# A decoder block with Strassen steps: a longer warm-up, two host units and the last branch unit with other step kinds, and operand fills spread over more ticks

## The chip, the core and the metric

The kernel runs on one core of one Trainium2 chip, as a single program. The metric is the device time of that program in microseconds (us). Three runs of the kernel before took 2395.96, 2396.16 and 2397.62 us; their median is 2396.16 us.

The engines go by their names in the profile: PE is TensorE (matmul; PEld is its weight load), DVE is VectorE, ACT is ScalarE, POOL is GpSimd and SP is SyncE. [...] A q behind a name (SPq, ACTq) marks what the engine's sequencer issues, DMAs above all.

## What is computed

One layer over 256 tokens of 4096 channels, float32:

```
h = rmsnorm(x, norm_w)
u_p, z_p, u_c, b_c, c_c, z_c, g = split(h @ w_in)     # 6 x 2048 and 8192 columns
pooled = trailing_mean(u_p, windows 2, 4, 8, 16) - u_p # by group of 512 channels
y_pool = (pooled @ pool_w) * pool_scale * silu(z_p)
v      = c_c * u_c
y_conv = b_c * (conv_b + sum_k conv_w[k] * shift(v, 2 - k)) * silu(z_c)
br     = y_pool @ w_branch[0], y_conv @ w_branch[1]
merged = sum over n of sigmoid(g_n + gate_b[n]) * br_n
out    = rmsnorm(x + merged @ w_out, final_norm_w)
```

Almost all of the work is in three matrix products with 256 rows: 4096 x 20480 (w_in), twice 2048 x 4096 (w_branch) and 4096 x 4096 (w_out).

## The kernel before

**Units and steps.** The columns of every weight matrix are cut into units of 1024 columns (class Unit, L332). The units run in this order: conv units cz0, cb0, cu0, cc0, cz1, cb1, cu1, cc1; pool units pz0, pu0, pz1, pu1; gate units g0_0, g1_0 to g0_3, g1_3; branch units b0_0, b1_0 to b0_3, b1_3; output units o0 to o3. A unit goes over its contraction dimension in steps of 256 rows (16 steps for w_in and w_out, 8 for a branch). One step multiplies a 256 x 256 block of the activations by a 256 x 1024 block of weights, 1 MB, which SP loads into one of three slots of `raw`.

Each float32 number is split into a rounded high part and a low part, and a product is done as high x high + high x low + low x high. A step has one of two kinds, given by a letter in the unit's text (L34 to L43):

- P, plain: eight products of 128 x 128 by 128 x 512, three matmuls each, 24 in all. ACT writes the weights' high parts into cells of `ring` (`highs`), DVE the low parts (`lows`).
- S, a Strassen step: seven products, 21 matmuls. DVE first makes four sums of the weights in `parts` (one addition of 128x1024, two of 128x512), ACT rounds the three used quarters of `raw` and the four sums, DVE subtracts for both.

Two more letters stand in the text of a host unit (HOST, L40): B is a step of banded matmuls for the trailing means, and M a step that multiplies them by pool_w. pz1 and g0_0 are the host units.

**The order of the work.** All of it is written out by hand: every engine call goes through `pin`, which keeps the program order of each engine. While PE's matmuls are issued, `pump` (L901 on) adds the preparation of the next steps to the other engines, up to four steps ahead (AHEAD), as far as ring cells and raw slots are free. After every six matmuls a `tick` (L927 on) takes one item from `queue`, which holds the epilogue of the unit before (activations, transposes, stores, with None as a pause), and calls `pop_fill` (L726).

**Activation operands.** The stationary side lies in `arena` (and `last_pair`), high and low part, for P operands the four blocks, for S operands also the sums that Strassen's method needs. For w_in it is made from x in the opening. Later ones, of y (branch) and of the merged result (output), are fills: class Fill, L695 on. A fill loads one block from DRAM by POOL's queue into one of two stage buffers, sa or sb; LANDING ticks later, when its place in the arena is free, `advance` does one phase in each tick: for an S operand the four subtractions of `sums_s` on DVE, then a copy on DVE (L687) and a subtraction on DVE; for a P operand a copy on ACT and a subtraction on DVE. If a step begins whose operand isn't ready, `run_step` forces the fill in front of it.

**End of a unit.** ACT evacuates the four banks of `sums` as they close (`evacuate`, L368), DVE combines the Strassen corners into them (`combine`, L389), and the next unit may write a bank only when it is evacuated.

**The convolution's taps** (`c_epi`, L490 on) run in the epilogue of cc0 and cc1, so beside the steps of cz1 and pz0: four lots of four instructions on DVE (128x255 and 128x254) with two on ACT, then a load of b's factor to E (`g_d`), six ticks later the product into Y, and two stores of Y to `y_d`.

**The opening** (L777 on). DVE clears `warm`, ACT starts the load of the parameters `par` and runs a small activation on `warm`, and PE multiplies `warm` ten times (WARM). SP loads the first weights in four parts of 256 KB, with the first block of x (256 KB, `fetch_x(0)`) issued after the first part. `x_direct` scales x on ACT (two instructions) and subtracts on DVE (two); for the first two steps ACT's `highs` and DVE's `lows` are done part by part.

Of the kernel before, what the change touches and what calls it, by code (L numbers as in the profile page):

```python
# [27 lines left out]
NRAW = 3  # L28
AHEAD = 4
TICK = 6  # L30
WARM = 10
TAIL = 3

SIX5 = "PPPPPSPSPSPSPSPS"  # L34
# [2 lines left out]
SIX4 = "PPPPSPSPSPSPSPSP"  # L37
SEVEN3 = "PPPSPSPSPSPSPSPS"
EIGHT = "PSPSPSPSPSPSPSPS"
HOST = "PPPBPPMMPPSPSSPSSPS"  # L40
OUT3 = "PSPSPSPSPSPSSPPP"
B0 = "PPPPSPSP"
B1 = "PSPSPSPP"  # L43


@with_exitstack
def hybrid_block(ctx: ExitStack, tc: tile.TileContext, x, xc, prm, rows_in, w_in, pool_w, w_branch, w_out, out):
    nc = tc.nc
# [4 lines left out]
    def act(dst, src, func=AF.Copy, **kw):  # L53
        return pin(nc.scalar.activation(dst, src, func, **kw))  # L54
# [4 lines left out]
    def mul(dst, a, b):  # L59
        return tt(dst, a, b, ALU.mult)  # L60
# [9 lines left out]

    def load(dst, src):
        return pin(nc.sync.dma_start(dst, src))

    def move(dst, src):
        return pin(nc.gpsimd.dma_start(dst, src))
# [129 lines left out]
    def highs(cells, src):  # L205
        for i, c in runs(cells):
            act(ring[:, c, 0], src[:, i])
# [14 lines left out]
    class Step:  # L222
# [7 lines left out]
        def first(self):  # L230
            if self.kind == "B":
                return []

            def rounded(cells):
                self.q = self.raw.rearrange("p (i c) -> p i c", i=4)
                self.cells = cells
                if self in steps[:2]:
                    for i in range(4):
                        highs(cells[i:i + 1], self.q[:, i:i + 1])
                else:  # L240
                    highs(cells, self.q[:, 0:len(cells)])

            return [(3 if self.kind == "S" else 4, None, rounded)]
# [145 lines left out]
    def combine(u):  # L389
        d = u.dst  # L390
        if u.s:
            corner_sums(u)
            assert u.cornered
            q = u.join.slot.rearrange("p (n t) c -> p t n c", n=2)
            d4 = d.rearrange("p t (n c) -> p t n c", n=2)
            if u.scaled:
                for t in range(2):
                    stt(d4[:, t], q[:, t], rin[:, t:t + 1], d4[:, t], ALU.mult, ALU.add)
            else:
                add(d4, d4, q)  # L400
            u.join.prepared = True
        u.flags["base"] = True
        if u.urgent:
            u.urgent()

# [25 lines left out]
    def put(dst, src):  # L431
        for k in range(2):
            move(dst[:, :, 1 - k], src.rearrange("p (q k) t -> p q k t", k=2)[:, :, k])

    def chan(tile_):
        return tile_.rearrange("p a n -> p (a n)").rearrange("p (b t) -> p b t", t=T)
# [4 lines left out]
    def gap(n):  # L441
        return [None] * n
# [5 lines left out]
    def make_ops(kinds):  # L448
# [2 lines left out]
    x_ops = make_ops([("P" if r[0] == "p" else "S", r) for r in x_regions])  # L451
    y_ops = [make_ops([("P", ("p", i)) for i in range(6)] + [("S", ("s", i)) for i in (0, 1)]),
             make_ops([("P", r) for r in (("p", 6), ("p", 7), ("q", 0), ("q", 1), ("q", 2))] +
                      [("S", ("s", i)) for i in (4, 5, 6)])]
    m_ops = make_ops([("P" if r[0] == "p" else "S", r) for r in x_regions])

    def sequence(text, np_, total, both):
# [24 lines left out]
    def conv_units(c, first):  # L482
        base = 2 * HALF + c * NU

        def b_epi(u):
            def copy(j):
                act(chan(Y)[:, 2 * j:2 * j + 2], bankview(j))
            return gap(6) + transposes(E, copy) + [lambda: move(g_d[c], Y)]

        def c_epi(u):  # L490
            def copy(j):
                if j == 3:
                    for i in range(4):
                        act(chan(E)[:, 2 * i:2 * i + 2], bankview(i))

            def taps(j):
                v, y = chan(E)[:, 2 * j:2 * j + 2], chan(Y)
                for i in range(2):
                    b = 2 * j + i
                    kb = 8 * c + b  # L500
                    act(y[:, b], v[:, i], AF.Identity, scale=tap_col(2, kb), bias=bias_col(kb))
                for i in range(2):
                    b = 2 * j + i
                    kb = 8 * c + b
                    for s in (1, 2):
                        stt(y[:, b, s:], v[:, i, 0:T - s], tap_col(2 - s, kb), y[:, b, s:], ALU.mult, ALU.add)

            items = gap(6) + pairs(transposes(E, copy)) + gap(1)
            for j, n in enumerate((1, 5, 7, 7)):
                items += gap(n) + [lambda j=j: taps(j)]  # L510
            return items + [lambda: move(E, g_d[c])] + gap(6) + [lambda: mul(Y, Y, E), lambda: put(y_d[1, c], chan(Y))]

        in_unit(f"cz{c}", base + 3 * HALF, lambda u: silu_y(), FIRST if first else SIX4, dst=Y)
        in_unit(f"cb{c}", base + HALF, b_epi, EIGHT).urgent = lambda: mul(E, E, Y)
        in_unit(f"cu{c}", base, lambda u: gap(2) + band_items(0) if c == 0 else [], SEVEN3, dst=Y)
        in_unit(f"cc{c}", base + 2 * HALF, c_epi, EIGHT).urgent = lambda: mul(E, E, Y)
# [115 lines left out]
    def branch_unit(n, c):  # L632
        def epi(u):
            if n == 0:
                return gap(8) + [lambda: mul(Y, E, Y)]
            turned = spare() if c < 3 else Y

            def gated():
                mul(E, E, spare())
                if c == 3:  # L640
                    last_pair["stack"].close()
                    open_last(F32R)
                    last_pair["again"] = True

            def copy(j):
                act(chan(turned)[:, 2 * j:2 * j + 2], bankview(j))

            def stored():
                put(m_d[c], chan(turned))
                merged[c] = now[0] + STORED  # L650
            return [lambda: move(spare(), gates_d[1, c])] + gap(6) + [gated, lambda: add(E, E, Y), None,
                lambda: c < 3 and move(Y, gates_d[0, c + 1])] + gap(3) + pairs(transposes(E, copy)) + [stored]

        text = B1 if n else B0
        u = Unit(f"b{n}_{c}", lambda i: w_branch[n, c, i], seq_y(text), y_ops[n], epi)
        u.urgent, u.lead, u.rotates = (lambda: None), 3, False
        units.append(u)
# [28 lines left out]
    def copy(dst, src):  # L686
        return pin(nc.vector.tensor_copy(dst, src))  # L687
# [7 lines left out]
    class Fill:  # L695
        def __init__(self, o, src, free, ready):
            self.o, self.free, self.ready, self.src = o, free, ready, src
            self.at = self.st = None
            self.phase = 0

        def fetch(self, st):
            self.at, self.st = now[0], st
            move(st[:, 4:8].rearrange("p o c -> p (o c)"), self.src)

        def advance(self):
            o, q = self.o, self.st[:, 0:self.o.n] if self.o.kind == "S" else self.st[:, 4:8]
            if self.phase == 0 and o.kind == "S":
                sums_s(self.st)
                self.phase = 1
            elif self.phase == 0:  # L710
                act(o.view[:, 0], q)
                self.phase = 2
            else:
                if self.phase == 1:
                    copy(o.view[:, 0], q)
                sub(o.view[:, 1], q, o.view[:, 0].bitcast(F32))
                self.phase = 3
                o.ready = True
                fills.remove(self)

    stages = [sa]
    fills = deque()
    now = [0]
    LANDING, STORED = 8, 7

    def pop_fill(force=None):  # L726
        now[0] += 1
        for f in list(fills):
            if f.at is not None and f.free() and (now[0] >= f.at + LANDING or f.o is force):
                f.advance()  # L730
                break
        used = [f.st for f in fills if f.at is not None]
        nxt = next((f for f in fills if f.at is None), None)
        if nxt is None or not nxt.ready():
            return
        st = next((q for q in stages if not any(q is u for u in used)), None)
        if st is not None:
            nxt.fetch(st)
# [38 lines left out]
    warm = op.tile([P, 2 * P], BF16, name="warm")  # L777
    pin(nc.vector.memset(warm, 0.0))
    pin(nc.scalar.dma_start(par, prm))
    act(warm[:, 0:2], warm[:, 2:4])  # L780
    make_identity(nc, ident)
    for _ in range(WARM):
        pin(nc.tensor.matmul(shared(3)[:, 0:2 * P], warm[:, 0:P], warm, start=True, stop=True))
# [22 lines left out]
    xt = Y.rearrange("p a n -> p (a n)").rearrange("p (s o c) -> p s o c", s=4, c=P)  # L806

    def fetch_x(j):
        load(xt[:, j % 4].rearrange("p o c -> p (o c)"), xc[first_order[j]])

    staged = [j for j in range(16) if x_ops[first_order[j]].kind == "S"]

# [71 lines left out]
    def issue_load(s):  # L884
        i = s.load_index
        r = raw[:, i % NRAW]
        if isinstance(s, Join):
            s.slot = r.rearrange("p (i c) -> p i c", i=4)
            return
        if i < 2:  # L890
            for k in range(4):
                load(r[:, k * NH:(k + 1) * NH], s.src[:, k * NH:(k + 1) * NH])
                if i == k == 0:
                    fetch_x(0)
        else:
            load(r, s.src)
        if i + 1 < 16:
            fetch_x(i + 1)
        s.raw = r
# [45 lines left out]
    def after_group(u, b, st):  # L945
# [14 lines left out]
            state["limit"] = state["now"] + u.lead  # L960
        pump()

    pump()

    def room(o):
# [166 lines left out]
```

## Time and profile before

| | us |
|---|---|
| median of three runs | 2396.16 |
| the profiled execution, its own time | 2395.7 |
| its span, first to last instruction | 2394.0 |
| matmuls in it | 10,515 |
| mean granted TensorE clock | 0.997 |
| DMA | 547 MB, 229 GB/s in the mean |

The rows that follow come from four views. The list of waits gives, for one engine, who released it, the total, the number and the longest. The timeline gives start, duration, engine, source line, operation, output <- input, shape, how many instructions are merged in the row, and in square brackets the engine's idle time before it with the releaser. The table of stretches gives for each stretch its length, then busy time and number of instructions of PE, PEld, DVE, ACT and POOL, then the granted clock, the DMA engines' share and GB/s. The chain of waits follows the end back from releaser to releaser. Durations overlap a little: a row of 33 matmuls lasts to the end of the last, while the next row starts when PE issues again.

### The profile page before, as it was taken

The numbers are of one execution on the slowest core, as the hardware profiler recorded it, in microseconds if no ns is written. First come the engines' busy times: TensorE is split into PE (matmuls) and PEld (weight loads), VectorE is DVE, ScalarE is ACT, GpSimd is POOL, SyncE is SP. The second block draws the span as 40 slices with busy tenths as digits, with TensorE's granted clock in tenths as the row PEclk, the third lists the DMA queues.
The fourth block names the chain that finished last, engine by engine and source line by source line (L and its number), as shares of the span: only waits on it lengthen the run. The fifth ranks groups of instructions, "written<-read, shape, count | busy, mean of one in ns | idle before, by whom it ended". The sixth has DMA issues, their size and how long they took to land. (4 is left out here: it accounts for less than half of the span.)

```text
span 2394.0 us, 26867 instructions
## 1 busy us (share of the span) xinstructions
PE 2372.0 (99%) x10515; PEld 1956.6 (82%) x10515; DVE 2136.9 (89%) x1770; ACT 1421.8 (59%) x1368; POOL 85.7 (4%) x147
## 2 busy tenths in 40 slices
PE   9999999999999999999999999999999999999998
PEld 7888888888888888888888888888888887888886
DVE  8779989988989969969998899889998798899998
ACT  6655556655556556556666656556665555556664
POOL 0000000000000000000000000001100001000000
PEclk9999999999999999999999999999999999999999
DMA  9656546655646645645766676677776766757767
GB/s 346 234 179 238 190 182 243 230 195 201 223 176 227 233 182 196 234 177 210 260 233 210 245 242 233 198 251 263 238 283 219 261 233 220 254 194 268 254 216 268
DMA packets 83391, 547.07 MB, mean 229 GB/s; under 512 B 9536, under 2 KB 9536, under 8 KB 22336
## 3 DMA queue, kind: packets, MB, share of 16 engines
q1 hardware_dynamic: 69824, 485.52, 56.0%
q0 software_dynamic: 13008, 58.73, 8.4%
q8 instruction: 82, 1.34, 0.2%
q10 hardware_dynamic: 432, 1.11, 0.1%
q14 instruction: 45, 0.37, 0.1%
HBM read 519.10 MB, written 26.21 MB: 228 GB/s over the span
## 5 line engine op out<-in xcount | busy, mean ns | idle before, releaser
L939 PE MATMUL sums<-ring,arena 128*128 128x512 f32 x7515 | 1751.5, 390 | 6.3 <-DVE ring L57 2.9
L939 PEld LDWEIGHTS sums<-ring,arena 128*128 128x128 f32 x7515 | 1409.2, 188 | 302.9 <-DVE ring L57 4.6
L57 DVE TENSOR_TENSOR ring<-raw,ring 128x1536 fp32r<-128x1536 f32 (+3 forms) x528 | 938.6, 1789 | 142.8 <-ACT ring L54 139.0
L54 ACT ACTIVATE ring<-raw 128x1536 fp32r<-128x1536 f32 (+3 forms) x528 | 790.7, 1515 | 460.3 <-PE sums L939 286.5
L54 ACT ACTIVATE ring<-parts 128x1024 fp32r<-128x1024 f32 (+1 forms) x402 | 400.6, 1010 | 391.4 <-DVE parts L57 331.6
L939 PE MATMUL shared<-ring,arena 128*128 128x512 f32 x2100 | 507.1, 390 | 1.2 <-DVE ring L57 1.2
L57 DVE TENSOR_TENSOR ring<-parts,ring 128x2048 fp32r<-128x2048 f32 (+3 forms) x224 | 434.8, 1953 | 42.6 <-ACT ring L54 41.8
L939 PEld LDWEIGHTS shared<-ring,arena 128*128 128x128 f32 x2100 | 395.2, 188 | 85.0 <-DVE ring L57 2.6
L57 DVE TENSOR_TENSOR parts<-parts,raw 128x512 f32<-128x512 f32 x378 | 261.9, 693 | 12.9
L57 DVE TENSOR_TENSOR parts<-raw 128x1024 f32<-128x1024 f32 x189 | 230.6, 1220 | 7.1 <-DMA raw<-in_w_in_dram 7.0
L939 PE MATMUL sums<-ring,last_pair 128*128 128x512 f32 x366 | 89.8, 396 | 0.0
L939 PEld LDWEIGHTS sums<-ring,last_pair 128*128 128x128 f32 x366 | 68.9, 188 | 16.5
L54 ACT ACTIVATE E<-sums,rin 128x512 f32<-128x512 f32 x56 | 36.3, 688 | 25.5 <-PE sums L939 25.4
L57 DVE TENSOR_TENSOR raw<-raw 128x512 f32<-128x512 f32 (+1 forms) x42 | 36.5, 869 | 10.3 <-ACT raw L54 9.3
L939 PE MATMUL shared<-ring,last_pair 128*128 128x512 f32 x168 | 41.6, 396 | 0.0
L939 PEld LDWEIGHTS shared<-ring,last_pair 128*128 128x128 f32 x168 | 31.6, 188 | 7.7
L54 ACT ACTIVATE raw<-shared 128x512 f32<-128x512 f32 x56 | 29.7, 610 | 0.4 <-DVE ring L57 0.2
L57 DVE TENSOR_TENSOR E<-E,last_pair 128x2048 f32<-128x2048 f32 x12 | 27.4, 2285 | 2.7 <-ACT E L54 2.7
L78 POOL DMA_DIRECT2D E<-in_rows_dram x16 | 13.9, 867 | 444.3 <-DVE E L69 442.2
L54 ACT ACTIVATE last_pair<-shared 128x512 f32<-128x512 f32 x44 | 24.1, 596 | 7.7 <-PE shared L422 7.0
L54 ACT ACTIVATE E<-sums 128x512 f32<-128x512 f32 x44 | 25.6, 599 | 4.0 <-PE sums L939 1.4
L54 ACT ACTIVATE Y<-shared 128x512 f32<-128x512 f32 x44 | 23.8, 598 | 4.8 <-PE shared L422 4.7
(120 smaller groups left out, 602.9 us busy)
## 6 DMA issues: line engine op xcount, KB each, us to landing
raw<-in_w_in_dram SPq DMA_DIRECT2D x318, 1024.0 KB, 4.8
raw<-in_w_branch_dram SPq DMA_DIRECT2D x64, 1024.0 KB, 4.9
raw<-in_w_out_dram SPq DMA_DIRECT2D x64, 1024.0 KB, 4.9
E<-in_rows_dram POOLq DMA_DIRECT2D x16, 512.0 KB, 8.1
gates_d<-E POOLq DMA_DIRECT2D x8, 1024.0 KB, 8.0
Y<-in_xc_dram SPq DMA_DIRECT2D x16, 256.0 KB, 6.6
raw<-in_pool_w_dram SPq DMA_DIRECT2D x4, 1024.0 KB, 6.8
Y<-gates_d POOLq DMA_DIRECT2D x4, 1024.0 KB, 5.8
```

What stands on the lines that cost most here:

```text
L54: return pin(nc.scalar.activation(dst, src, func, **kw))
L57: return pin(nc.vector.tensor_tensor(out=dst, in0=a, in1=b, op=op))
L78: return pin(nc.gpsimd.dma_start(dst, src, accum_op=ALU.add))
L939: pin(nc.tensor.matmul(ps, lhs, rhs, start=n == 0, stop=n == u.total[b] - 1))
```

## The change

- WARM is 18 instead of 10. The small activation on `warm` is gone.
- The first block of x is loaded by ACT's DMA queue (`feed`), ahead of the first `pump`; SP issues the four parts of the first weights one behind the other.
- In the first step, the high part of the first quarter of the weights is a copy on DVE instead of an activation.
- HOST has nine P and seven S instead of ten and six; its S steps begin one place sooner.
- The last branch unit, b1_3, has the text B1_LAST: S at places 2 and 5 instead of 2, 4 and 6. Operand 5 of that branch is used by a P step there, and is laid in the region s6, which has room for all eight blocks.
- The pauses ahead of the four lots of taps are 1, 7, 9, 9 ticks instead of 1, 5, 7, 7. The product goes into E instead of Y and is stored from E.
- Fills: an S operand's copy is on ACT; at least four ticks lie between its sums and the copy, and one between copy and subtraction; for five ticks after a unit's `combine` (QUIET), `advance` starts no phase but the copy of an S operand.

```diff
-WARM = 10
+WARM = 18
...
-HOST = "PPPBPPMMPPSPSSPSSPS"
+HOST = "PPPBPPMMPSPSSPSSPSS"
...
+B1_LAST = "PSPPSPPP"
...
+    def feed(dst, src):
+        return pin(nc.scalar.dma_start(dst, src))
...
                     for i in range(4):
-                        highs(cells[i:i + 1], self.q[:, i:i + 1])
+                        if self is steps[0] and i == 0:
+                            copy(ring[:, cells[0], 0], self.q[:, 0])
+                        else:
+                            highs(cells[i:i + 1], self.q[:, i:i + 1])
...
         u.flags["base"] = True
+        quiet[0] = now[0] + QUIET
...
-                      [("S", ("s", i)) for i in (4, 5, 6)])]
+                      [("S", ("s", i)) for i in (6, 4, 5)])]
...
-            for j, n in enumerate((1, 5, 7, 7)):
+            for j, n in enumerate((1, 7, 9, 9)):
                 items += gap(n) + [lambda j=j: taps(j)]
-            return items + [lambda: move(E, g_d[c])] + gap(6) + [lambda: mul(Y, Y, E), lambda: put(y_d[1, c], chan(Y))]
+            return items + [lambda: move(E, g_d[c])] + gap(6) + [lambda: mul(E, E, Y), lambda: put(y_d[1, c], chan(E))]
...
-        text = B1 if n else B0
+        text = (B1_LAST if c == 3 else B1) if n else B0
...
-            self.phase = 0
+            self.phase = self.due = 0
...
-        def advance(self):
+        def advance(self, force):
             o, q = self.o, self.st[:, 0:self.o.n] if self.o.kind == "S" else self.st[:, 4:8]
+            if not force and (now[0] < self.due or (self.phase != 1 and now[0] < quiet[0])):
+                return False
             if self.phase == 0 and o.kind == "S":
                 sums_s(self.st)
-                self.phase = 1
-            elif self.phase == 0:
+                self.phase, self.due = 1, now[0] + 4
+            elif self.phase < 2:
                 act(o.view[:, 0], q)
-                self.phase = 2
+                self.phase, self.due = 2, now[0] + 1
             else:
-                if self.phase == 1:
-                    copy(o.view[:, 0], q)
                 sub(o.view[:, 1], q, o.view[:, 0].bitcast(F32))
-                self.phase = 3
                 o.ready = True
                 fills.remove(self)
+            return True
...
-    now = [0]
-    LANDING, STORED = 8, 7
+    now, quiet = [0], [0]
+    LANDING, STORED, QUIET = 8, 7, 5
...
-                f.advance()
-                break
+                if f.advance(f.o is force):
+                    break
...
-    act(warm[:, 0:2], warm[:, 2:4])
...
-        load(xt[:, j % 4].rearrange("p o c -> p (o c)"), xc[first_order[j]])
+        (load if j else feed)(xt[:, j % 4].rearrange("p o c -> p (o c)"), xc[first_order[j]])
...
-                if i == k == 0:
-                    fetch_x(0)
...
+    fetch_x(0)
     pump()
```

## The prediction

> **What bounds the kernel now.** The page comes first, then what TensorE (PE) waited for.
>
> ```profile
> span 2394.0 us, 26867 instructions
> PE 2372.0 (99%) x10515; PEld 1956.6 (82%) x10515; DVE 2136.9 (89%) x1770; ACT 1421.8 (59%) x1368; POOL 85.7 (4%) x147
> ...
> PE sums L939 <- DVE ring L57: 2.9, 1, 2.9
> PE shared L783 <- ACT warm L54: 2.8, 1, 2.8
> PE sums L939 <- ACT ring L54: 1.8, 1, 1.8
> PE sums L939 <- ACT Y L54: 1.3, 2, 0.9
> ```
>
> The 10,515 matmuls leave PE idle for 22 us in all, half of it behind the last matmul. So the change can win only by fewer matmuls, by removing the few waits listed (us in total, times, longest), or by running fewer matmuls at a low clock. VectorE (DVE), 89% busy, is the next bound: where it is full, its work decides when PE stalls.
>
> Next, the pace of PE at one place where it stalls:
>
> ```profile
> 2111.02 2.88 PE L939 MATMUL shared<-ring,arena 128*128 128x512 f32 x12
> 2113.74 7.64 PE L939 MATMUL sums<-ring,arena 128*128 128x512 f32 x33
> 2121.22 1.07 PE L939 MATMUL shared<-ring,arena 128*128 128x512 f32 x4
> 2123.49 2.11 PE L939 MATMUL shared<-ring,arena 128*128 128x512 f32 x8 [1.20 <-DVE ring L57]
> ```
>
> Twelve matmuls take 2113.74 - 2111.02 = 2.72 us, 0.2267 us each. The four at 2121.22 should have been followed at 2122.13; the next came at 2123.49, so 1.4 us were lost.
>
> The longest wait costs more than the 2.9 us listed:
>
> ```profile
> 2026.66 1.75 PE L939 MATMUL sums<-ring,arena 128*128 128x512 f32 x7
> 2031.34 2.50 PE L939 MATMUL sums<-ring,arena 128*128 128x512 f32 x5 [2.93 <-DVE ring L57]
> 2033.64 4.68 PE L939 MATMUL shared<-ring,arena 128*128 128x512 f32 x12
> 2038.15 1.08 PE L939 MATMUL sums<-ring,arena 128*128 128x512 f32 x4
> ...
> 2030.60:2034.00 3.40, 2.66 (x6) 2.15 (x7) 3.40 (x3) 3.40 (x3) 0.54 (x1) 0.50 0.39 123
> 2034.00:2037.40 3.40, 3.40 (x9) 2.64 (x8) 3.40 (x3) 1.03 (x3) 0.00 (x0) 0.50 0.77 282
> ```
>
> The seven matmuls at 2026.66 end their issue at 2028.25. Then 5 + 12 matmuls, worth 3.9 us, fill the time to 2038.15, which is 9.9 us: **6.0 us lost**, half as the wait, half because the granted clock (third column from the right) fell to 0.50 in it.
>
> **The change part by part.**
>
> *Last branch unit (B1_LAST), fills spread.* DVE in front of that wait:
>
> ```profile
> 2022.03 2.28 DVE L57 TENSOR_TENSOR Y<-E,Y 128x2048 f32<-128x2048 f32 x1
> 2024.23 1.01 DVE L57 TENSOR_TENSOR sb<-sb 128x128 f32<-128x128 f32 x4
> 2025.28 0.63 DVE L687 CAST arena<-sb 128x896 fp32r<-128x896 f32 x1
> 2025.94 1.09 DVE L57 TENSOR_TENSOR arena<-sb,arena 128x896 fp32r<-128x896 f32 x1
> 2026.95 1.22 DVE L57 TENSOR_TENSOR parts<-raw 128x1024 f32<-128x1024 f32 x1
> 2028.20 1.42 DVE L57 TENSOR_TENSOR parts<-parts,raw 128x512 f32<-128x512 f32 x2
> 2029.53 1.75 DVE L57 TENSOR_TENSOR ring<-raw,ring 128x1536 fp32r<-128x1536 f32 x1
> 2031.80 2.28 DVE L57 TENSOR_TENSOR ring<-parts,ring 128x2048 fp32r<-128x2048 f32 x1
> ```
>
> A Strassen step costs DVE 1.22 + 1.42 + 1.75 + 2.28 = 6.7 us and PE 21 matmuls, 4.8 us. A plain step costs DVE one pass of 128x2048, 2.28 us, and PE 24 matmuls, 5.4 us. The unit's third Strassen step is the one waited for. With two, and the second one place later, DVE has 4.4 us less to do by then and PE 0.7 us more; a fill (2024.23 to 2027.0) loses its CAST of 0.63 us to ScalarE. That is 5.7 us of room against a wait of 3.1: it goes, and the low clock with it: **-6.0** (between -6.0 and, if a wait too short to lower the clock stays, -3). PE pays 3 matmuls: +0.7.
>
> The fill's copies on ScalarE (ACT), 12 of about 0.9 us, go to an engine busy 59%. A copy stands four ticks behind the sums it needs, so ACT should not block on it; were it to, the evacuations queued behind it would be late (the last rival).
>
> In the first output unit the chain of waits runs through DVE from 2092.6 to 2123.5, with four copies of this kind in it:
>
> ```profile
> 2098.10 0.62 DVE arena L687
> ...
> 2119.48 0.64 DVE arena L687
> ```
>
> Four times 0.63 is 2.5 us, more than the 1.4 us wait at 2123.49: **-1.4** (0 if the later fills bunch, -1.7 with a 0.2 us wait ahead of the transposes at 2070).
>
> *Host units.* Each of the two trades a plain step for a Strassen step: PE 2 x 3 x 0.2267 = **-1.4**, DVE +4.4 us each. DVE has that time ahead of it, and the new order starts on Strassen steps one place sooner:
>
> ```profile
> 880.00:900.00 20.00, 20.00 (x98) 16.58 (x97) 14.44 (x12) 12.10 (x14) 3.46 (x7) 1.00 0.47 177
> 400.00:420.00 20.00, 20.00 (x89) 16.12 (x87) 19.86 (x15) 9.33 (x8) 1.51 (x3) 1.00 0.79 288
> ```
>
> 5.6 us of DVE (third busy figure) are free in 880 to 900. But the built order puts a Strassen step's adds between the two multiplies that the mix's transposes need: about 2.2 us later where 2.0 were free, +0.1 in each: **+0.2** (0 to +3, were the room used up).
>
> *Taps later.* The second row shows DVE full in the stretch where the taps, and 2.28 us for the product, stand. They move by 6 ticks (8 us) but stay in the unit, ahead of its last step; the sum of DVE work before the wait on "ACT Y" (1.3 us in two units) is the same. Moving work inside a full queue shortens nothing: PE will not stall in the middle but at the end. The y stores, now read from E, leave 8 us later and meet other weight loads. I take **-0.4** (-2 to +1).
>
> *The opening.* Its rows:
>
> ```profile
> 0.90 0.17 DVE L778 MEMSET warm<- 128x128 uint32 x1 [0.90 <-PEq L1121]
> ...
> 1.24 1.28 ACT L54 ACT_TABLE_LOAD   x1 [1.24 <-PEq L1121]
> 1.25 0.42 SPq L72 DMA_DIRECT2D Y<-in_xc_dram  x1
> ...
> 2.54 0.20 ACT L54 ACTIVATE warm<-warm 128x2 bf16<-128x2 bf16 x1
> ...
> 2.79 2.31 PE L783 MATMUL shared<-warm 128*128 128x256 bf16 x10 [2.79 <-ACT warm L54]
> ...
> 5.39 0.91 ACT L54 ACTIVATE arena<-Y,par 128x256 fp32r<-128x256 f32 x2 [2.65 <-DMA Y<-in_xc_dram]
> 5.93 0.88 DVE L69 SCALAR_TENSOR_TENSOR arena<-Y,par,arena 128x256 fp32r<-128x256 f32 x2 [4.86 <-ACT arena L54]
> 6.20 2.17 ACT L54 ACTIVATE ring<-raw 128x512 fp32r<-128x512 f32 x4
> ...
> 6.87 16.20 PE L939 MATMUL sums<-ring,arena 128*128 128x512 f32 x63 [1.76 <-ACT ring L54]
> ...
> 16.44 0.22 DVE L687 CAST extra<-sa 128x128 fp32r<-128x128 f32 x1
> ...
> 6.87:9.90 3.03, 3.03 (x7) 2.45 (x8) 3.03 (x6) 3.00 (x7) 0.00 (x0) 1.00 1.04 364
> ```
>
> Today the small activation draws the table load to 1.24, while nothing else can run. The change deletes it. In the built order of the changed kernel ACT's wait for x stands ahead of the table load, so the 1.28 us come after x has landed, and ACT's two scalings, its roundings and DVE's first work queue behind them. The first rounding moves to DVE, which is in order: it comes behind the two low parts of x. So the first matmul comes at x's landing (5.4) + 1.28 + 0.91 + 0.44 + the copy of 512 columns, 0.4 between the CASTs of 0.22 (128 columns) and 0.63 (896) = 8.4, against 6.87. On ACT's queue x is issued as early as before, but its packets share the engines with the later weight parts instead of going ahead of them: landing -0.2 to +0.9, I take +0.4. SP issues those parts 0.4 us sooner, which ends no wait, since x decides. First matmul: 8.8, **+2.0**.
>
> Seven matmuls in 6.87 to 9.90 (13.4 at full pace) show half speed, though the clock column knows no event there: 1.45 us lost today. Eighteen small matmuls from about 1.1, at 0.21 each, end at 5.1. The gap to 8.8 is longer than the one at 2028, after which the clock was low for 6.8 us. So the extra warm matmuls warm nothing that lasts. I count 2.0 us lost at low clock (0.3, DVE's own pace, to 3.1): +0.5 net of today's 1.45. Opening: **+2.4** (0.2 to 4.0).
>
> [...]
>
> [...]
>
> **Sum.** -6.0 + 0.7 - 1.4 - 1.4 + 0.2 - 0.4 + 2.4 = -5.9. The profiled execution took 2395.7 us around its span of 2394.0; the median of the runs shown is 2396.16. 2395.7 - 5.9 = **2389.8 us**.
>
> **Rivals.**
> 1. *The clock holds through the opening.* Eighteen matmuls lift it and it does not fall by 8.8; then 0.3 instead of 2.0 us are lost: 2388.1. For it: 1.4 us idle at 2122 left the clock up. Against it: 3.1 us at 2028 did not. Chance 0.10.
> 2. *The wait at 2028 moves instead of going.* The fills wait 5 ticks after a unit's sum and 4 between phases, so the same DVE work falls later, where a new wait of 3 us lowers the clock again: +6.0, 2395.8. For it: DVE is full there in most stretches. Against it: the unit itself has 4.4 us less. Chance 0.12.
> 3. *Slower: fills come too late.* A Strassen fill holds one of two stage buffers some 5 ticks (7 us) longer. If the last fills of the first output unit are not done when their step begins, they are forced in front of it: load (about 4 us), sums 1.0, copy 0.9, subtraction 1.1 = 7 us with PE idle, and 3 us of low clock: +10 for one (2399.8), +20 for two (2410). It decides from two on. Against it: in the built order the last two fills' sums stand some 8 us ahead of their use. Chance 0.04 for two, 0.02 for one.
> 4. *The host units stall*, 1.5 us each at their ends: 2392.8. Chance 0.10.
>
> **Numbers.** My forecast has 0.62: 2389.8, by the bounds of its terms 2386 to 2393. The range for 8 in 10, with rivals 1 and 4 and part of 2: **2385.5 to 2394**. About 0.2% (4.8 us) is what a measurement of this kernel can tell from no change: below 2391.4 is faster. Of my forecast 0.85 lies there, of rival 1 all, of rival 4 a fifth: faster 0.65; slower, above 2401, 0.04; the rest, 0.31, within.
>
> **What would show it.** Right: PE's first L939 matmul at 8 to 9.5 us with the table load after x; no PE wait and clock 1.00 from 2000 to 2130; DVE without L687 CASTs there; 10,520 matmuls; the "ACT Y" waits still there. Wrong: a first matmul before 7 us, a stretch of half clock after 20 us, a wait on the arena or last_pair in the first output unit, or any PE wait over 1 us in the host units.

## The result, and the profile after

The changed kernel takes **2387.52 us** (median of five runs, 2386.46 to 2387.59) against 2396.52 us before (five runs, 2395.96 to 2397.94): a ratio of 0.996, 95% interval 0.9945 to 0.9974. It is 9.0 us faster; the forecast was 2389.8. Its profiled execution took 2387.53 us.

The head of the page, and then the whole list of PE's waits, of the changed kernel:

```profile
span 2385.8 us, 26931 instructions
PE 2368.8 (99%) x10520; PEld 1957.0 (82%) x10520; DVE 2132.8 (89%) x1779; ACT 1435.7 (60%) x1393; POOL 85.1 (4%) x147
```

```profile
PE sums L944 <- DVE ring L695: 4.4, 1, 4.4
PE shared L790 <- DVE warm L786: 1.1, 1, 1.1
PE shared L430 <- DVE E L58: 0.2, 1, 0.2
```

There are 10,520 matmuls, as forecast. After the first large matmul, 0.2 us is all that the list has left. The 2.9 and 1.2 us waits of before are gone, and the "ACT Y" waits too (1.3 us), which the forecast expected to stay. The one longer wait, 4.4 us, lies in the opening, where before had waits of 2.8 and 1.8.

PE's timeline where its longest wait was, and where it waited at 2123:

```profile
2023.65 2.88 PE L944 MATMUL shared<-ring,arena 128*128 128x512 f32 x12
2026.37 18.98 PE L944 MATMUL sums<-ring,arena 128*128 128x512 f32 x83
```

```profile
2118.02 5.78 PE L944 MATMUL sums<-ring,last_pair 128*128 128x512 f32 x24
2123.63 2.23 PE L944 MATMUL sums<-ring,arena 128*128 128x512 f32 x9
```

Eighty-three matmuls run in one row, 18.98 us at 0.2267 us each, where before 5 + 12 matmuls took 9.9 us. From 2118.02 to 2123.63 are 24 matmuls, 5.61 us or 0.234 us each: no wait.

The opening, in the timeline:

```profile
1.12 4.02 PE L790 MATMUL shared<-warm 128*128 128x256 bf16 x18 [1.12 <-DVE warm L786]
1.24 0.45 ACTq L76 DMA_DIRECT2D Y<-in_xc_dram  x1
...
6.37 1.28 ACT L55 ACT_TABLE_LOAD   x1 [6.37 <-DMA Y<-in_xc_dram]
7.67 0.91 ACT L55 ACTIVATE arena<-Y,par 128x256 fp32r<-128x256 f32 x2
...
9.01 0.42 DVE L695 CAST ring<-raw 128x512 fp32r<-128x512 f32 x1
...
9.58 17.30 PE L944 MATMUL sums<-ring,arena 128*128 128x512 f32 x63 [4.43 <-DVE ring L695]
```

x lands at 6.37, a microsecond later than the 5.39 of before, though its load is issued as early. Only then does the table load run, 1.28 us, and the first matmul comes at 9.58 instead of 6.87.

The table of stretches tells the rest. The stretches are cut where the trace records a change of clock, at 5.24, 8.65 and 15.47, and halfway between the last two:

```profile
1.83:5.24 3.41, 3.31 (x16) 2.02 (x14) 0.00 (x0) 0.00 (x0) 0.00 (x0) 1.00 0.84 236
5.24:8.65 3.41, 0.00 (x0) 0.00 (x0) 0.44 (x2) 2.26 (x4) 0.00 (x0) 1.00 1.05 398
8.65:12.06 3.41, 2.48 (x6) 2.03 (x7) 3.38 (x8) 3.41 (x8) 0.00 (x0) 0.50 0.99 345
12.06:15.47 3.41, 3.41 (x9) 2.64 (x9) 3.38 (x8) 1.97 (x4) 0.00 (x0) 0.50 1.03 409
15.47:18.88 3.41, 3.41 (x16) 2.80 (x16) 3.31 (x8) 2.79 (x4) 0.00 (x0) 1.00 0.99 372
```

At 5.24, after the 18 small matmuls (PE busy for 3.31 us of the first row), the first recorded change is to 1.00. PE is idle all through the second row (0.00 us), and at 8.65, 0.9 us before the first large matmul, the clock falls to 0.50. The first 14 matmuls, those up to 15.47, ran at half pace (9 in 3.41 us against 16 afterwards). Summed over the gaps between matmuls up to 17 us, 2.85 us are lost there, against 1.53 before.

### The profile page after: what moved, and what is told of

Read it like the earlier page. It is cut to its first block, busy times and chain, and to the rows that moved or that the text cites. A ratio compares the mean times of both kernels' runs of the same rounds, so it can differ in the third digit from the quotient of the medians.

```text
span 2385.8 us, 26931 instructions
## 1 busy us (share of the span) xinstructions
PE 2368.8 (99%) x10520; PEld 1957.0 (82%) x10520; DVE 2132.8 (89%) x1779; ACT 1435.7 (60%) x1393; POOL 85.1 (4%) x147
## 4 chain that ended last, share of the span: by engine, by line
PE 99%; DVE 0%; ACT 0%; DMA 0%; issue 0%; DVEq 0%; ACTq 0%
PE sums L944 75%; PE shared L944 22%; PE shared L610 1%; PE shared L430 1%; DMA Y<-in_xc_dram 0%; DVE E L58 0%; DVE raw L58 0%; PE shared L586 0%; DVE E L70 0%; ACT raw L55 0%; PE shared L587 0%; ACT E L55 0%; PE shared L589 0%; ACT ring L55 0%; ACT L55 0%
## 5 line engine op out<-in xcount | busy, mean ns | idle before, releaser
L58 DVE TENSOR_TENSOR ring<-raw,ring 128x2048 fp32r<-128x2048 f32 (+3 forms) x542 | 939.1, 1745 | 138.2 <-ACT ring L55 134.6
L58 DVE TENSOR_TENSOR E<-E,Y 128x2048 f32<-128x2048 f32 x13 | 29.7, 2285 | 0.1
```

What stands on the lines that cost most here:

```text
L58: return pin(nc.vector.tensor_tensor(out=dst, in0=a, in1=b, op=op))
```

## The experiments

In all of them "before" ran on the same chip: 2396.51, 2396.75 and 2396.59 us in the three sets. The changed kernel itself was timed only in the set of the result (before: 2396.52 us), so a difference against it compares two sets. Fractions of a microsecond between medians of 5 to 11 runs are not more than a hint; the ratio to before is known to about 0.001 (2 us). Where the text speaks of what PE lost in a stretch, it is the time between the starts of its large matmuls (128x512) beyond 0.2267 us each, in the one profiled execution of each kernel.

### Last branch unit and fills: alone and together

`e5_last_only` is the kernel before with B1_LAST and its region; `e6_fills_only` has only the fills' rules; `e9_last_and_fills` has both.

```diff
+B1_LAST = "PSPPSPPP"
...
-        text = B1 if n else B0
+        text = (B1_LAST if c == 3 else B1) if n else B0
```

```diff
+        quiet[0] = now[0] + QUIET
...
+            if not force and (now[0] < self.due or (self.phase != 1 and now[0] < quiet[0])):
+                return False
...
+                self.phase, self.due = 1, now[0] + 4
+            elif self.phase < 2:
                 act(o.view[:, 0], q)
...
-                if self.phase == 1:
-                    copy(o.view[:, 0], q)
```

> The kernel before with the text PSPPSPPP for the last branch unit and the other order of its Strassen regions alone. My theory: DVE has 4.4 us less to do by the third place waited for, so the wait of 3.1 us and the low clock behind it go: -6.0 + 0.7 = -5.3 us, 2391.2 us; the wait of 1.4 us in the first output unit stays. Rival (the fills are the cause, the step only shows it): a wait of 1 to 3 us stays at about 2028, 2393 to 2396 us.

> The kernel before with the spreading of the fills alone (copy on ACT, pauses between phases, five ticks of quiet after a unit's sum). My theory: 0.63 us for each fill's copy does not pay for 3.1 us at 2028, so a wait of some 2 us stays there, low clock after it or not by its length, while the wait of 1.4 us in the first output unit goes: -1.5 to -5 us, 2391.5 to 2395 us. Rival (spreading alone is enough): -7.5 us, 2389 us.

> The kernel before with two parts of the change together: the last branch unit's two Strassen steps and the spread fills. In the profile of the fills alone three waits are left that the changed kernel doesn't have, between 2020 and 2080 us: 1.04 + 1.29 + 0.78 = 3.1 us. Theory: the third Strassen step is what they stand on, so that the last unit's text removes what the fills leave: 2392.05 - 3.1 + 0.7 for three more matmuls = 2389.6, and no wait of PE over 0.5 us from 2000 to 2150. Rival: both parts remove the same wait, so that the text adds nothing to the fills but its three matmuls: 2392 to 2393, with waits of some 2 us left between 2020 and 2080.

| | us (lowest to highest, runs) | ratio, 95% interval | against before |
|---|---|---|---|
| e5, last unit alone | 2394.66 (2393.76 to 2396.54, 11) | 0.9991, 0.9983 to 1.0 | -2.1 |
| e6, fills alone | 2392.05 (2390.99 to 2393.69, 11) | 0.9981, 0.9972 to 0.999 | -4.7 |
| e9, both | 2388.53 (2387.97 to 2389.45, 6) | 0.9966, 0.9954 to 0.9978 | -8.1 |

PE's timeline at the old wait, of e5, e6 and e9 in turn:

```profile
2027.60 1.07 PE L940 MATMUL sums<-ring,arena 128*128 128x512 f32 x4
2030.38 14.81 PE L940 MATMUL sums<-ring,arena 128*128 128x512 f32 x64 [1.71 <-DVE ring L58]
```

```profile
2030.66 1.09 PE L940 MATMUL shared<-ring,arena 128*128 128x512 f32 x4
2032.51 2.10 PE L940 MATMUL shared<-ring,arena 128*128 128x512 f32 x8 [0.76 <-DVE ring L57]
...
2047.20 20.70 PE L940 MATMUL sums<-ring,arena 128*128 128x512 f32 x90 [1.02 <-ACT E L54]
```

```profile
2024.53 2.88 PE L941 MATMUL shared<-ring,arena 128*128 128x512 f32 x12
2027.25 23.06 PE L941 MATMUL sums<-ring,arena 128*128 128x512 f32 x101
```

Neither alone removes the stall. The last unit's text leaves a wait of 1.7 us, because a fill still stands undivided in front of the step's work on DVE; e5's timeline of DVE:

```profile
2024.72 1.01 DVE L58 TENSOR_TENSOR sb<-sb 128x128 f32<-128x128 f32 x4
2025.76 0.63 DVE L688 CAST arena<-sb 128x896 fp32r<-128x896 f32 x1
2026.43 1.09 DVE L58 TENSOR_TENSOR arena<-sb,arena 128x896 fp32r<-128x896 f32 x1
2027.43 0.68 DVE L58 TENSOR_TENSOR arena<-sa,arena 128x512 fp32r<-128x512 f32 x1
2028.04 4.55 DVE L58 TENSOR_TENSOR ring<-raw,ring 128x2048 fp32r<-128x2048 f32 x3
```

The fills' rules alone leave 0.8 and 1.0 us (which of these rules does how much, no run separates). Both together leave nothing there, and e9's list of waits has no entry from 1690 us to the end. The theory of e9, that each removes what the other leaves, holds; its rival (2392 to 2393) falls. Together they gave 1.1 us more than the theory said. The 5.3 us that the forecast's working gave to e5 alone were not there: e5's rival, a wait that stays at about 2028, came true.

### The taps: pauses, product, stores

`e3_taps_only` is before with the whole part (pauses 1, 7, 9, 9 and the product in E). `e10_pauses_only` has only the pauses. `e4_put_late` has the old pauses, the product in E, and the stores six items further back in the queue:

```diff
-            ... gap(6) + [lambda: mul(Y, Y, E), lambda: put(y_d[1, c], chan(Y))]
+            ... gap(6) + [lambda: mul(E, E, Y)] + gap(6) + [lambda: put(y_d[1, c], chan(E))]
```

> The kernel before with the taps' part of the change alone (longer pauses, product in E, stored from E). The prediction's theory (moving DVE work inside a full queue shortens nothing): 2396.1 us, -0.4 us, PE still waits at the ends of cz1 and pz0. Rival, from the trace of after: the y stores no longer run against the last weight loads of the unit, and the wait for the evacuation goes: -2.5 us, 2394.0 us.

> The kernel before with the pauses of the taps as they were, the product in E, and only the two y stores six ticks later. If the stores' traffic against the weight loads is the cause, this has nearly all of the gain of the taps' part: -1.5 to -2.5 us, and the wait on ACT Y goes. If the order of DVE's work is the cause, it stays at 2396.5 us with the waits of before.

> The kernel before with the taps' pauses 1, 7, 9, 9 and nothing else: the product stays in Y and is stored from Y. Theory: the order of VectorE's work beside the unit's last steps is what counts, so the pauses alone give all that the whole part gave: 2394.5, and no wait on ACT Y near 431 and 770 us. Rival: the product in E is needed too (Y's stores and the unit's evacuation into Y are then on different tiles): 2396.5, as for the kernel before, with the waits on ACT Y left.

| | us (lowest to highest, runs) | ratio, 95% interval | against before |
|---|---|---|---|
| e3, whole part | 2394.45 (2393.06 to 2395.61, 11) | 0.9992, 0.9983 to 1.0 | -2.1 |
| e4, stores later in the queue | 2396.85 (2395.2 to 2401.12, 11) | 1.0002, 0.9993 to 1.0011 | +0.3 |
| e10, pauses alone | 2394.03 (2393.01 to 2395.8, 11) | 0.9989, 0.9981 to 0.9998 | -2.6 |

By the medians the pauses alone give as much as the whole part, and e3's rival, 2394.0, was nearer than its theory, 2396.1. These intervals are wide; the traces say it more sharply. From 400 to 440 and from 720 to 780 us PE lost 2.0 to 3.6 us together in the six kernels with the old pauses and 0.3 to 0.6 in the eight with the new ones. Of the six, e4, which has the product in E, lost 2.1: alone the product in E shows no gain. And e4 did not do what it was made for. POOL's timeline, of e4 and then of e10:

```profile
412.15 1.49 POOL L75 DMA_DIRECT2D y_d<-E  x2 [12.21 <-DVE E L57]
```

```profile
419.93 1.49 POOL L75 DMA_DIRECT2D y_d<-Y  x2 [10.01 <-DVE Y L57]
```

In e4 the stores left at 412.15, where they left before (412.23). Here a pause in the queue only placed an instruction in its engine's program; POOL had nothing else to do and issued the stores 0.3 us after DVE's product ended: at 411.85 in e4, at 419.63 in e10. Here only what moves the product moves the stores. So e4 tests nothing about the stores.

What the pauses do is seen in ACT's longest waits from 410 to 432 us, before and in e10:

```profile
ACT ring L54 <- DVE parts L57: 5.6, 2, 5.2
ACT ring L54 <- DMA raw<-in_w_in_dram: 3.1, 2, 2.0
```

```profile
ACT ring L54 <- DVE parts L57: 4.6, 3, 3.8
ACT ring L54 <- PE sums L939: 2.8, 2, 1.9
```

Before, ACT waits 3.1 us for weights that are late. In e10 no wait for a load is left. The packets in the trace, added up in KB by stretch and queue:

```
us         before: weights  POOL's DMAs    e10: weights  POOL's DMAs
412-415                  0          488             104          696
415-418                464          336             920            0
418-421                768          200             768            0
421-424                760            0             256          848
424-427                184            0               0          176
```

Before, the y stores (1024 KB from 413 to 420) run beside two weight loads, issued at 414.17 and 418.43, and the second has its last packets after 424. In e10 the same two loads (413.20, 417.46) run alone but for the end of the load of E, issued at 409.36; the second has landed at 422.3, and most of the stores fall into the gap behind them, since the next load is issued only at 426.34. Of the 3.2 us by which the second load lands later before (425.5), 1.0 is its later issue and 2.2 its longer way (7.1 us against 4.85). An estimate from these rows: without the 2.2 it would have landed at 423.3, and ACT, busy until 423.56, would not have waited for it. After that ACT's evacuation is no longer late, and PE's 0.94 us wait "<-ACT Y" at 431 is not there. PE's rows of before, then of e10:

```profile
424.31 5.78 PE L939 MATMUL sums<-ring,last_pair 128*128 128x512 f32 x24
431.02 7.12 PE L939 MATMUL sums<-ring,arena 128*128 128x512 f32 x30 [0.94 <-ACT Y L54]
```

```profile
425.18 5.78 PE L939 MATMUL sums<-ring,last_pair 128*128 128x512 f32 x24
430.80 6.99 PE L939 MATMUL sums<-ring,arena 128*128 128x512 f32 x30
```

That the stores' place beside the loads is the cause, and not the place of DVE's 2.28 us product itself, is argued from these packets; the two move together in every kernel here, and no run separates them.

The second place, near 765 us, went only part of the way. From 745 to 772 ACT's waits for loads come to 4.5 us before, 2.8 in e10 and 1.3 in e3, and e10 still has a wait of 0.35 us "<-ACT Y" at 764.59. So e10's expectation held at 431 and not at 770.

### The host units

`e7_host_only` is before with the new HOST; `e11_old_host` is the changed kernel with the old one.

```diff
-HOST = "PPPBPPMMPPSPSSPSSPS"
+HOST = "PPPBPPMMPSPSSPSSPSS"
```

> The kernel before with the new HOST text alone: six matmuls fewer. My theory: -1.2 to -1.4 us, 2395.2 us, no new PE wait in the host units. Rival (DVE's 4.4 us more stall PE at the end of the units): 0 to +3 us.

> The changed kernel with the old order of the host units: ten plain and six Strassen steps in each instead of nine and seven. Theory: six matmuls fewer are worth 6 x 0.2267 = 1.36 us where no wait takes them back, so without them 2387.5 + 1.4 = 2388.9. Rival: the host units are worth what they gave alone on the kernel before, 0.2 us: 2387.7.

e7: 2396.58 us (2395.46 to 2397.18, 11 runs), ratio 0.9998, 0.9989 to 1.0007: 0.2 us gained, a miss. e11: 2388.88 us (2387.41 to 2389.54, 6 runs), ratio 0.9969, 0.9958 to 0.998: 1.4 us above the changed kernel, as six matmuls of 0.2267 us give. Neither has a wait in the host units: from 860 to 1140 us PE lost 0.8 us in every kernel here, so the six matmuls are saved in e7 too. Its profiled execution lost the gain in places that the edit does not touch: 3.0 us at half pace in the opening against 1.5 before, and a wait of 1.7 us at 2123 against 1.2. Whether its other executions did the same is not settled, and the interval of its ratio alone reaches from -2.6 to +1.7 us.

### The opening

`e1_open_before` is the changed kernel with the opening of before. `e2_early_table` is the changed kernel with a small activation on a tile of its own, issued on ACT behind x's load:

```diff
     fetch_x(0)
+    seed = op.tile([P, 4], BF16, name="seed")
+    pin(nc.vector.memset(seed, 0.0))
+    act(seed[:, 0:2], seed[:, 2:4])
     pump()
```

`e8_open_best` has x back on SP's queue and the first high part back on ACT, that small activation right behind the load of `par`, and 26 small matmuls (WARM). `e12_x_first` is e8 with x issued ahead of the first weights.

> The changed kernel with the opening of the kernel before (10 warm matmuls, the small activation, x by SP, the first high part on ACT). My theory: the opening costs the change 2.7 us of a later first matmul (9.58 against 6.87) and 1.2 us more at low clock, so this kernel is 3.9 us faster than the changed one: 2383.6 us, first L-matmul of the first step at 6.9 us. Rival (the opening is free because the first weights bound it anyway): 2387.5 us.

> The changed kernel with one small activation on a tile of its own behind the issue of x, so that the table load runs before x lands; the warm matmuls do not wait for it. My theory: the table load is 1.3 us of the later first matmul, so it comes at 8.3 instead of 9.58 us and the kernel ends at 2386.2 us, give or take 1.5 us by where the clock rises. Rival (the queue of x is the whole cause): first matmul still at 9.6 us, 2387.5 us.

> The changed kernel with x by SP behind the first quarter of the weights, the first high part on ACT, the table load drawn early by an activation on its own tile, and 26 warm matmuls that start at 1.1 us and end close to the first step. My theory: first matmul at 6.9 us, and no or at most 1.5 us at low clock after it because PE is never idle long enough: 2381.5 to 2383 us, faster than the changed kernel with the opening of before. Rival (the clock falls or doesn't rise whatever PE did before): as with the opening of before, 2383.6 us.

> As the best opening so far, with x's first block issued ahead of the first weights on SP's queue. Theory: the opening is bound by what the DMA engines bring in, so a first matmul 0.4 us earlier (6.4 instead of 6.84) is waited away before 20 us, where PE now stands 1.1 us for weights that land at 15.1: 2384.1, unchanged within 0.3. Rival: the first matmul sets the end: 2383.7, with the wait at 19.36 no longer than now.

| | us (lowest to highest, 5 runs) | ratio, 95% interval | first large matmul | against the changed kernel |
|---|---|---|---|---|
| e1, old opening | 2384.63 (2383.73 to 2385.33) | 0.9951, 0.9938 to 0.9965 | 6.85 | -2.9 |
| e2, table early | 2385.8 (2385.15 to 2387.49) | 0.9958, 0.9945 to 0.997 | 8.33 | -1.7 |
| e8, best of both | 2384.12 (2383.36 to 2384.42) | 0.9946, 0.9933 to 0.996 | 6.84 | -3.4 |
| e12, x first | 2384.87 (2384.32 to 2385.37) | 0.9953, 0.994 to 0.9965 | 6.50 | -2.6 |

The change to the opening costs 2.9 us (e1). Its first large matmul is 2.7 us later, and 1.25 us of that (9.58 - 8.33) is the table load that stands behind x (e2). Another 1.0 is x itself: with x on SP's queue it lands a microsecond sooner (by 5.36 in e8, at 6.37 in the changed kernel). The last 0.4 is the first high part: from ACT's first scaling of x to the first large matmul it is 1.91 us in e2, with the copy on DVE, and 1.48 in e8, with ACT's rounding. e1's theory, 3.9 us, was a miss by 1.0: it took 1.2 us for the difference at low clock, but e1 lost 2.4 us there, only 0.5 less than the changed kernel. ACT's timeline of e8:

```profile
1.24 1.28 ACT L55 ACT_TABLE_LOAD   x1 [1.24 <-PEq L1128]
2.54 0.20 ACT L55 ACTIVATE seed<-seed 128x2 bf16<-128x2 bf16 x1
5.36 0.91 ACT L55 ACTIVATE arena<-Y,par 128x256 fp32r<-128x256 f32 x2 [2.62 <-DMA Y<-in_xc_dram]
```

In e8 the first large matmul follows the end of the small ones (5.5) by 1.4 us, where in the changed kernel it was 4.4 us, and the clock column stands at 1.00 in every stretch up to 18 us. Its stretches, cut at the one change that is recorded there, at 3.87:

```profile
0.46:3.87 3.41, 2.75 (x13) 1.94 (x14) 0.18 (x2) 1.49 (x2) 0.55 (x4) 1.00 0.45 107
3.87:7.28 3.41, 2.03 (x16) 1.57 (x15) 1.35 (x3) 1.92 (x5) 0.00 (x0) 1.00 1.02 357
7.28:10.69 3.41, 3.41 (x17) 2.80 (x16) 3.41 (x8) 3.04 (x7) 0.00 (x0) 1.00 1.00 350
```

From 7.28 on 17 matmuls run in 3.41 us, full pace, and up to 17 us less than 0.2 us is lost where e1 loses 2.4. It is nearly the same in e12: 49 matmuls from 6.50 take 11.44 us, against 11.41 for the 49 from 6.84 in e8. Yet e8 is only 0.5 us better than e1. Where it goes, in PE's waits of the first 30 us of e8 and then of e12:

```profile
PE sums L946 <- ACT ring L55: 1.4, 1, 1.4
...
PE sums L946 <- DVE ring L58: 1.1, 1, 1.1
```

```profile
PE sums L946 <- DVE ring L58: 1.7, 1, 1.7
```

A new wait stands at 19.36 in e8: ACT waits 1.6 us for weights that are there at 15.06, rounds them by 16.98, and DVE makes their low parts by 19.30. The DMA engines' share is 0.99 to 1.04 in each stretch of 3 us from 3 to 18 us of e8. In e12 the first matmul is 0.34 us earlier still, ACT waits 1.6 us for the same weights, until 15.36, and PE's wait grows from 1.1 to 1.7 us; PE resumes at 19.66. So these two openings are bound by what the DMA engines bring in up to there, and in e12 the faster start is waited away, as e12's theory had it; the rival's 2383.7 was not seen. The time, though, is 0.75 us above e8's and not unchanged within 0.3: 0.3 of it is the later 19.66, and its profiled execution has a wait of 0.7 us on an evacuation near 2040 (0.2 in e8) that no part of the edit explains. e8's own expectation, 2381.5 to 2383, was a miss for the same reason: it did not count the wait at 19.36.

e8 is faster than both kernels: 3.4 us below the changed one, 12.6 below its own set's before. It takes all parts of the change but those in the opening, of which it keeps only a longer warm-up.

## Why the prediction was right or wrong

| step | forecast | measured |
|---|---|---|
| last unit and fills, with three more matmuls and the wait at 2123 | -6.0 + 0.7 - 1.4 = -6.7 | -8.1 (e9) |
| host units | -1.4 + 0.2 = -1.2 | -1.4 (e11) |
| taps | -0.4 | -2.1 (e3), -2.6 (e10) |
| opening | +2.4 | +2.9 (e1) |
| sum | -5.9 | -8.7, with e3's taps |

The intervals behind these medians are about 2 us to either side, as wide as the differences. What decides below are the waits and gaps in the traces.

**Right.** The sign, the place of the gain and its mechanism: the wait at 2028 went and the low clock with it, the wait at 2123 went, PE ran without a stall from 2000 to 2130 at a clock of 1.00, and the first large matmul came late because of the table load and x's later landing (at 9.58, just past the 8 to 9.5 that the prediction gave as its sign). None of the four rivals came about: the clock did not hold through the opening (it fell at 8.65), the stall at 2028 did not move, no fill was forced, and the host units did not stall. Within the first step the weights were off: of the 5.7 us of room that the forecast counted, it gave 4.4 to the last unit and 0.63 to the fill. Alone the unit gave 2.1 us (e5) and the fills' rules 4.7 (e6).

**Taps: the step that failed.** The prediction said: "Moving work inside a full queue shortens nothing: PE will not stall in the middle but at the end. The y stores, now read from E, leave 8 us later and meet other weight loads." The sum of DVE's work is the same, but as far as the packets show, DVE's work was not what ended last. The wait "<-ACT Y" had a late weight load behind it: ACT waited 3.1 us for loads there, and the move takes the stores away from the two loads they ran beside; it brings them beside no others but the last 256 KB of the second. The row that would have said so, ACT's wait for a DMA, stood in the profile of before. And the 1.3 us of the two listed waits were too small a measure: summed over its gaps from 400 to 440 and from 720 to 780, PE lost 2.8 us before and 0.3 after, so the whole part lay at or past the lower of the bounds, -2 to +1.

**Last unit and fills: mis-sized by 1.4.** The forecast was worked from one execution, in which PE's gaps at 1702, 1745 and 2060 to 2080 come to 0.8 and 0.4 us. In the profiled executions of e3 and e4, which are the kernel before in these places, they are larger: 1.0 and 1.1 us near 1702, 1.9 and 1.9 near 2068. In e9 the first are zero and the last is 0.4. In the other kernels with the old fills (e5, e7, e10) these places cost 2.4 to 4.2 us together. The profiled execution of before was 0.8 us below the median of five, and it underrated small waits that come and go.

**Opening: mis-sized by 0.5, in two places.** x landed 1.0 us later, not 0.4 and just over the bound of 0.9, so the first matmul was at 9.58 instead of 8.8. The low clock cost 2.85 us instead of the 2.0 that the author estimated; today's 1.45 (1.53 by the gaps) is no fixed price either, since the profiled executions of the other kernels with ten small matmuls lost 1.4 to 3.0 us there. Against e1's 2.4, the later first matmul and the low clock make 2.7 + 0.5 = 3.2 us, near the 2.9 measured. "So the extra warm matmuls warm nothing that lasts" was right for the changed kernel, whose clock fell at 8.65; in e8, with 26 of them, less than 0.2 us was lost up to 17 us.

By these the forecast is off by -1.4 - 1.7 - 0.2 + 0.5 = -2.8, and +0.8 because it started from an execution below the median of before: 2387.8, against 2387.5 measured.

## What to carry to other kernels

Before a wait on an engine's result is priced by that engine's load, follow it back one more step: here late transfers, for which ACT waited 3.1 us, stood behind it. Two parts of a change that each left a stall when alone (1.7 us in e5, 0.8 and 1.0 in e6) removed it together (e9), so price such parts together. A pause in this program placed an instruction for its own engine, not in time; POOL's stores left 0.3 us after their data were ready, so move the producer. Let a table load run while the first transfer is under way (behind it the load cost 1.25 us here), and let a warm-up reach up to the first real matmul (the clock stayed up over a gap of 1.4 us in e8 and fell in one of 4.4); after that this kernel's opening is bound by the bytes (a DMA share of 0.99 to 1.04 in e8).

## What the runs showed of the hardware

**After the same wait the low clock lasted 6.8 us in one execution and 3.4 in another.** The wait of 2.9 us near 2028 was followed by 6.8 us at a clock of 0.50 before and by 3.4 in e3; in all, 6.0 and 4.9 us were lost. e10 also lost 6.0 us there, e4 4.7. The rows of before, then of e3, cut at their own changes:

```profile
2027.17:2030.58 3.41, 1.24 (x6) 0.70 (x4) 3.34 (x4) 1.93 (x2) 0.54 (x1) 1.00 0.30 77
2030.58:2033.99 3.41, 2.65 (x6) 2.15 (x7) 3.41 (x3) 3.41 (x3) 0.54 (x1) 0.50 0.39 120
2034.00:2037.41 3.41, 3.41 (x9) 2.64 (x8) 3.41 (x3) 1.04 (x3) 0.00 (x0) 0.50 0.77 281
```

```profile
2027.78:2031.19 3.41, 1.51 (x7) 1.25 (x8) 3.41 (x4) 3.14 (x3) 0.44 (x1) 1.00 0.19 48
2031.19:2034.60 3.41, 3.41 (x9) 2.35 (x8) 3.41 (x3) 1.52 (x1) 0.10 (x1) 0.50 0.89 348
```

In the 3.41 us ahead of the fall PE was busy for 1.24 us before and for 1.51 in e3. Before, the clock stayed at 0.50 through a stretch with 2.65 us of PE and the next one with 3.41; in e3 it was back at 1.00 after one with 3.41. Behind e5's wait of 1.7 us the 64 matmuls of the row took 14.81 us, 0.231 us each: no low clock. In the changed kernel's opening the clock changed at 5.24, 8.65 and 15.47, 3.41 and 6.82 us apart. What made the low clock last longer in one execution than in the other is not shown by any run.

**x's landing changed with its queue and its place.** Issued at 1.24 us on ACT's queue, beside four weight parts on SP's, x landed at 6.37; issued at 1.25 on SP's queue between the first part and the second, it landed by 5.36 (e8). Issued at 0.80 ahead of all parts (e12), it landed by 3.80. On SP's queue x also went ahead of three parts; no run has it behind them, so queue and place are not separated.
